# A router kernel on one core: a trip counter for the spare products, one address wrap per trip, and rows 52 to 62 in seven loads

## The chip, the cores and the metric

The kernel runs on one core of a Trainium2 chip. The metric is the device time of one execution in microseconds; the lower the better. A core has five engines with their own instruction queues: TensorE (PE in the profile; its weight loads are PEld), VectorE (DVE), ScalarE (ACT), GpSimd (POOL) and SyncE (SP). They wait for each other by semaphores only.

## The reference

Router logits of 8,192 tokens against 8 experts, and a softmax over the 8:

```python
# x: (16, 512, 1024) float32, router_weights: (1024, 8) float32
logits = np.matmul(x, router_weights)
exp_logits = np.exp(logits - np.max(logits, axis=-1, keepdims=True))
return (exp_logits / np.sum(exp_logits, axis=-1, keepdims=True)).astype(np.float32)
```

The work is the reading of x, 33.6 MB, and little arithmetic: each token is 1,024 numbers against an 8-column matrix.

## The kernel before

**Rows.** The tokens lie on 128 partitions with 64 tokens each. "Row" j means token j of every partition, so a row is 128 tokens of 1,024 numbers, 0.5 MB of float32. There are 64 rows (`J`), cut into 8 chunks (`KO`) of 128 columns.

**Loads.** `LOADS` lists how many rows each load carries: 4, then four of 8, four of 4, three of 2, five of 1, in order of rows; row 63 comes last in three `PIECES` of 4, 2 and 2 chunks. The first load (rows 0 to 3) goes through SyncE as float32 into `x_f32`, and ScalarE casts it. All the others are issued by GpSimd (L187, L200) one after the other at the start and are turned to bfloat16 on the way into `x_all`, where every row has its own place: no load waits for a buffer. SyncE waits for each load in turn (L175) and adds its number of rows to the semaphore `s_in`, which TensorE takes down by one before each row (L232).

**A row on TensorE.** The row has to be turned, so that the 1,024 columns lie on partitions: eight transposes (`loop_turn`), five into the PSUM tile `ptv`, three into `pts`. VectorE copies `ptv` to `xTv` (L421), ScalarE copies `pts` to `xTs` (L375). Then eight products with the weights `w_bf` accumulate the row's logits in `lg` (`multiply`). There are two buffers of each, so TensorE turns row j+1 before it multiplies row j.

**The loop.** Rows 1 to 62 are 31 trips (`TRIPS`) of two rows, written as basic blocks that only TensorE runs: `rows_turn` turns an odd row and multiplies the even one before it, `rows_even` turns an even row and branches back (L323), and `rows_multiply` runs two spare products and multiplies the odd row. The addresses are in registers: `r_x[c]` is where chunk c of the next row lies, `r_l` where the logits go. After each row all are advanced (L243, L247), and `r_l` is wrapped by a mask (L246), because `lg` has 16 places. In the trace neighbouring additions appear as one record, FUSED_REGOPS.

**Spare products.** `fill` multiplies constants (`filler`) into a bank that nobody reads. Two of them run in every trip. In addition the block `rows_spare` runs six in a straight line. It is entered after an odd row where the address in `r_x[0]` has certain bits (L319 masks it into `r_t`, L320 compares). `x_all` is laid at such an address (`ROW_AT`) that this holds just before rows 12, 20, 28 and 36, each the first row of the load that follows a load of eight.

**The softmax.** Every eight rows VectorE and ScalarE do the softmax of a group (peak, difference, exponential, sum, reciprocal, scaling) between their copies. After the loop come row 63 in pieces, the last four rows one by one, and two stores of the output by SyncE (L178, L180).

Of the kernel before, what the change touches and what calls it, by code (L numbers as in the profile page):

```python
# [11 lines left out]
def kernel(  # L12
# [6 lines left out]
    nc = tc.nc  # L19
    P = 128  # L20
    B, S, D = x.shape
# [3 lines left out]
    KO = D // P  # L25
    J = M // P
# [6 lines left out]
    bf16 = mybir.dt.bfloat16  # L33
    Exp = mybir.ActivationFunctionType.Exp
    X = mybir.AxisListType.X
    ALU = mybir.AluOpType

    LOADS = [4] + [8] * 4 + [4] * 4 + [2, 2, 2] + [1] * 5  # L40
    PIECES = [4, 2, 2]
    G, SKIP = 8, 4
    TRIPS = 31
# [5 lines left out]
    DONE = ends[-1]  # L49
    assert sum(LOADS) == J - 1 and sum(PIECES) == KO and ends[-1] == J - ALONE  # L50
    VN, SN = 5, 3

    LOT, SPARE = 8, 6
    ROW_AT = 32 - LOADS[0] - LOT
    assert LOADS[1:5] == [LOT] * 4 and 64 - ROW_AT == LOADS[0] + LOT * 5

    place = [16640]  # L60

    def sb(name, shape, dtype):
        size = mybir.dt.size(dtype)
        for n in shape[1:]:
            size *= n
        at = place[0]
        place[0] = -(-(at + size) // 64) * 64
        return nc.alloc_sbuf_tensor_at(name, shape, dtype, offset=at).ap()

    def ps(name, shape, dtype):  # L70
        return nc.alloc_psum_tensor(name, shape, dtype).ap()

    x_f32 = sb("x_f32", [P, LOADS[0], D], fp32)
    place[0] = X_AT = ROW_AT * D * 2
    xa = sb("x_all", [P, J, D], bf16)
    identity = sb("identity", [P, P], bf16)
    ident = sb("ident", [P, P], fp32)
    w8 = sb("w8", [KO, P, N], fp32)
# [31 lines left out]
    s_w = nc.alloc_semaphore("s_w")  # L110
    s_ld = [sem(f"s_ld{i}") for i in range(len(LOADS))]
    s_z = [sem(f"s_z{i}") for i in range(len(PIECES))]
# [21 lines left out]

    first = [sum(LOADS[:i]) for i in range(len(LOADS))]
    cols = [sum(PIECES[:i]) for i in range(len(PIECES))]
# [61 lines left out]
    for i, n in enumerate(PIECES):  # L198
        c = slice(cols[i] * P, (cols[i] + n) * P)
# [5 lines left out]
    pe = nc.tensor  # L205
    r_x = [pe.alloc_register(f"rx{c}") for c in range(KO)]
    r_l = pe.alloc_register("rl")
    r_t = pe.alloc_register("rt")
    for c, r in enumerate(r_x):

        pe.reg_mov(r, X_AT + D * 2 + c * P * 2 + (P - 1) * 2)
    pe.reg_mov(r_l, LG_AT + 256 * (SKIP - 1))

    def at(ap, like, r):
        return mybir.RegisterAccessPattern(
            ap=ap, dtype=like.dtype, memsetref=like.tensor.name + "_set",
            regref=r.name, is_regloc_offset=False, reg_ap_offset=r.name,
            const_ap_offset=0, const_sub_tensor_id=0,
        )

    def again(like, **k):
        return pe.add_instruction(copy.replace(like, name=f"I-{nc.next_id()}", **k))

    def turn_ap(b, c):
        return (ptv if c < VN else pts)[b][:, c if c < VN else c - VN, :]
# [4 lines left out]
    def loop_turn(b):  # L230

        pe.wait_ge(s_in, 1).then_inc(s_in, -1)  # L232
        for c in range(KO):
            t = again(
                turn_like,
                ins=(turn_like.ins[0], at([[J * D, P], [1, P]], xa, r_x[c])),
                outs=(pe.lower_ap(turn_ap(b, c), opt=False),),
            )
            if c == VN - 1:
                t.then_inc(s_tv, 1)  # L240
            if c == KO - 1:
                t.then_inc(s_ts, 1)
        pe.reg_add(r_l, r_l, 256)  # L243
        for c in range(KO):
            if c == KO // 2:
                pe.reg_alu(r_l, r_l, -4097, ALU.bitwise_and)  # L246
            pe.reg_add(r_x[c], r_x[c], D * 2)  # L247

    def turn(j):
        for c in range(KO):  # L250
            t = pe.transpose(turn_ap(j % 2, c), xa[:, j, c * P:(c + 1) * P], identity)
            if c == VN - 1:
                t.then_inc(s_tv, 1)
            if c == KO - 1:
                t.then_inc(s_ts, 1)
        return t

    def multiply(b, dst):

        for c in range(KO):  # L260
            if c == 0:
                pe.wait_ge(s_c[b], 2).then_inc(s_c[b], -2)
            if dst is None:
                m = again(
                    mult_like,
                    ins=(
                        pe.lower_ap(w_bf[:, c, :], opt=False),
                        pe.lower_ap(chunk(b, c), opt=False, for_matmul_weights=True),
                    ),
                    outs=(at([[2 * G * 64, P], [1, N]], lg, r_l),),  # L270
                    start_tensor_calc=(c == 0),
                    stop_tensor_calc=(c == KO - 1),
                )
            else:
                m = pe.matmul(  # L275
                    dst, lhsT=chunk(b, c), rhs=w_bf[:, c, :],
                    start=(c == 0), stop=(c == KO - 1),
                )
            if c == KO - 1:
                m.then_inc(s_p, 1)  # L280

    def fill():
        return pe.matmul(spare, lhsT=filler[:, 0:P], rhs=filler, start=True, stop=True)  # L283
# [5 lines left out]
    for n in range(N):  # L289
        t = pe.transpose(w_ps[:, n, :], w8[:, :, n], ident[0:KO, 0:KO])  # L290
# [2 lines left out]
    mult_like = fill().ins  # L293
    pe.wait_ge(s_idb, 1)
    pe.wait_ge(s_in, 1).then_inc(s_in, -1)  # L295
    turn_like = pe.transpose(turn_ap(0, 0), xa[:, 0, 0:P], identity).ins  # L296
    turn(0)
    pe.wait_ge(s_wb, 1)


# [4 lines left out]
    only_pe = OrderedEngineSet([pe.engine])  # L305
    nc.br("rows_turn", engines=only_pe)
    with nc.body("rows_spare", valid_engines=only_pe):
        for _ in range(SPARE):
            fill()
        pe.br("rows_even")  # L310
    with nc.body("rows_multiply", valid_engines=only_pe):
        fill()
# [3 lines left out]
    with nc.body("rows_turn", valid_engines=only_pe):  # L316
        loop_turn(1)
        multiply(0, None)
        pe.reg_alu(r_t, r_x[0], (64 + 32 + LOT - 1) * D * 2, ALU.bitwise_and)  # L319
        pe.br_eq(r_t, 32 * D * 2, on_true="rows_spare", on_false="rows_even")  # L320
    with nc.body("rows_even", valid_engines=only_pe):
        loop_turn(0)
        pe.br_lt(r_x[0], left_of(TRIPS - 1), on_true="rows_multiply", on_false="rows_done")  # L323
# [238 lines left out]
```

## Time and profile before

| | |
|---|---|
| median of 4 runs | 85.64 us (85.54 to 85.68) |
| profiled execution, its own time | 85.68 us |
| its span, first to last instruction | 84.4 us |
| PE busy / PEld busy | 69.8 us (83%) / 54.6 us (65%) |
| DVE busy / ACT busy | 39.4 us (47%) / 38.0 us (45%) |
| HBM read | 33.59 MB, 401 GB/s over the span |
| spare products in the trace | 85 records |
| loads issued by GpSimd | 16 and 3 pieces, from 2.7 to 14.0 us |

The profile's times are counted from the first instruction of the span. A line of its timeline gives the start, the time to the last end of the merged instructions, the engine, the line of the kernel, the operation, the tiles and the count; in brackets stands the idle time of the engine before it and what ended it. PEq is TensorE's sequencer: `PEq L232` is the wait for a row. A line of the waits gives the total in us, the number and the longest. A matmul's own duration is a latency: neighbours overlap, so what counts is the distance between starts. The busy time of the spare products is therefore more than what they take from others.

### The profile page before, as it was taken

The page shows a single profiled execution, that of the slowest core. Times are in us where ns is not written, and L with a number is a line of the kernel's source. Part 1 is how long each engine was busy: PE and PEld are TensorE (multiplying, and loading weights), DVE is VectorE, ACT ScalarE, POOL GpSimd, SP SyncE. Part 2 cuts the span into 40 slices and gives each one's busy share as a digit, 9 for nine tenths or more (in the row PEclk, how much of TensorE's full clock was granted, in tenths as well). Part 3 has the DMA queues.
Part 4 walks back from the last instruction along what each step waited for, and adds up shares of the span by engine and source line. Part 5 has one row for each costly group of instructions (what it writes and reads, how often), then busy time and mean ns, then how long its engine had stood idle before and what let it go on. Part 6 is the DMA issues. An engine that isn't in the chain of part 4 may idle for free. (4 is left out here: it accounts for less than half of the span.)

```text
span 84.4 us, 3030 instructions
## 1 busy us (share of the span) xinstructions
PE 69.8 (83%) x1118; PEld 54.6 (65%) x1118; DVE 39.4 (47%) x114; ACT 38.0 (45%) x81; POOL 11.3 (13%) x26
## 2 busy tenths in 40 slices
PE   0070376889999999999996999999999999999870
PEld 0040364759786788748881787678878888877650
DVE  0030042224364277527560476347657646765662
ACT  0600868323264255525451265426556544655580
POOL 0699996000000000000000000000000000000000
PEclk9999999999999999999999999999999999999999
DMA  5999979988998999799969999999999999999930
GB/s 148 388 458 264 225 148 249 249 186 186 249 249 171 202 249 241 155 225 249 233 148 229 198 233 202 233 202 225 206 214 200 214 216 214 204 208 211 187 117 11
DMA packets 3184, 18.12 MB, mean 215 GB/s; under 512 B 488, under 2 KB 1000, under 8 KB 2032
## 3 DMA queue, kind: packets, MB, share of 16 engines
q0 software_dynamic: 2736, 15.73, 90.4%
q1 hardware_dynamic: 432, 2.36, 7.4%
q10 hardware_dynamic: 16, 0.03, 0.2%
HBM read 33.59 MB, written 0.26 MB: 401 GB/s over the span
## 5 line engine op out<-in xcount | busy, mean ns | idle before, releaser
L421 DVE COPY xTv<-ptv 128x640 bf16<-128x640 bf16 x63 | 30.9, 491 | 33.0 <-PE ptv L296 27.7
L375 ACT COPY xTs<-pts 128x384 bf16<-128x384 bf16 x63 | 30.0, 476 | 35.2 <-PE pts L296 34.8
L296 PE MATMUL ptv<-identity,x_all 128*128 128x128 bf16 x311 | 29.3, 228 | 7.0 <-PEq L295 3.6
L283 PE MATMUL spare<-filler 128*128 128x512 bf16 x85 | 25.9, 402 | 0.1
L296 PEld LDWEIGHTS ptv<-identity,x_all 128*128 (+1 forms) x311 | 19.3, 100 | 9.1 <-issue 8.5
L296 PE MATMUL pts<-identity,x_all 128*128 128x128 bf16 x186 | 21.8, 229 | 0.0
L283 PEld LDWEIGHTS lg<-w_bf,xTv 128*128 128x128 bf16 x305 | 15.9, 99 | 8.1 <-issue 1.6
L283 PE MATMUL lg<-w_bf,xTv 128*128 128x8 bf16 x305 | 16.8, 168 | 0.0
L296 PEld LDWEIGHTS pts<-identity,x_all 128*128 x186 | 14.1, 104 | 0.0
L283 PE MATMUL lg<-w_bf,xTs 128*128 128x8 bf16 x183 | 13.2, 166 | 0.0
L283 PEld LDWEIGHTS spare<-filler 128*128 128x128 bf16 x85 | 6.1, 101 | 4.8 <-issue 0.6
L283 PEld LDWEIGHTS lg<-w_bf,xTs 128*128 128x128 bf16 x183 | 9.0, 96 | 0.0
L187 POOL DMA_DIRECT2D x_all<-in_x_dram x16 | 8.6, 598 | 2.2 <-POOLq L149 2.2
L361 ACT CAST x_all<-x_f 128x1024 bf16<-128x1024 f32 x4 | 4.0, 1044 | 5.2 <-ACTq L378 5.2
L290 PE MATMUL lg<-ident,w 8*128 8x8 f32 x8 | 1.0, 251 | 4.7 <-PEq L288 4.7
L290 PEld LDWEIGHTS lg<-ident,w 8*128 8x128 f32 x8 | 0.9, 197 | 4.7 <-issue 4.7
L441 DVE TENSOR_REDUCE mx<-lg 128x8 f32 x8 | 1.8, 224 | 4.4 <-DVEq L491 4.0
L412 DVE CAST identity<-ident 128x128 bf16<-128x128 f32 x1 | 0.5, 519 | 4.6 <-POOL ident L193 4.6
L364 ACT ACTIVATE ev<-ex 128x64 f32<-128x64 f32 x8 | 2.1, 256 | 1.4 <-DVE ex L441 0.8
L377 ACT ACT_TABLE_LOAD x1 | 1.3, 1283 | 2.2 <-PEq L149 2.2
L457 DVE TENSOR_REDUCE ssum<-ev 128x8 f32<-128x64 f32 x8 | 1.7, 218 | 0.0
L441 DVE TENSOR_TENSOR ex<-lg,mx 128x64 f32<-128x64 f32 x8 | 1.7, 215 | 0.0
(41 smaller groups left out, 16.0 us busy)
## 6 DMA issues: line engine op xcount, KB each, us to landing
x_all<-in_x_dram POOLq DMA_DIRECT2D x4, 2048.0 KB, 27.5
x_all<-in_x_dram POOLq DMA_DIRECT2D x4, 1024.0 KB, 51.6
x_f<-in_x_dram SPq DMA_DIRECT2D x1, 2048.0 KB, 8.5
x_all<-in_x_dram POOLq DMA_DIRECT2D x3, 512.0 KB, 62.0
x_all<-in_x_dram POOLq DMA_DIRECT2D x5, 256.0 KB, 66.1
out_dram<-out_all SPq DMA_DIRECT2D x1, 240.0 KB, 2.0
x_all<-in_x_dram POOLq DMA_DIRECT2D x1, 128.0 KB, 67.7
x_all<-in_x_dram POOLq DMA_DIRECT2D x2, 64.0 KB, 67.5
```

The lines of the kernel that those rows point to most:

```text
L187: nc.gpsimd.dma_start(out=xa[:, first[i]:first[i] + r, :], in_=x_rows[:, first[i]:first[i] + r, :]).then_inc(s_ld[i], 16)
L283: return pe.matmul(spare, lhsT=filler[:, 0:P], rhs=filler, start=True, stop=True)
L290: t = pe.transpose(w_ps[:, n, :], w8[:, :, n], ident[0:KO, 0:KO])
L296: turn_like = pe.transpose(turn_ap(0, 0), xa[:, 0, 0:P], identity).ins
L361: act.copy(xa[:, k, :], x_f32[:, k, :]).then_inc(s_cast, 1)
L364: return act.activation(ev, ex, func=Exp).then_inc(s_ev, 1)
L375: act.copy(xTs[j % 2], pts[j % 2][:, 0:SN, :]).then_inc(s_c[j % 2], 1)
L377: act.preload_act_table(Exp)
L412: dve.tensor_copy(out=identity, in_=ident).then_inc(s_idb, 1)
L421: dve.tensor_copy(out=xTv[j % 2], in_=ptv[j % 2][:, 0:VN, :]).then_inc(s_c[j % 2], 1)
L441: return dve.add_instruction(kind(name=f"I-{nc.next_id()}", engine=dve.engine, **k))
L457: dve.reduce_sum(ssum[:, :, 0], ev, axis=X).then_inc(s_d, 1)
```

## The change

- `LOADS` ends in 3, 2, 2 and four of 1 instead of 2, 2, 2 and five of 1: rows 52 to 62 come in seven loads instead of eight.
- `r_l` is wrapped only after odd rows (`b == 1`), so once in a trip.
- `r_t` becomes a counter. It starts at `STEP` = 3, loses 3 after each odd row, and below 1 the trip goes to `rows_spare`. There two spare products run, `r_t` gains 4, and the block repeats until `r_t` reaches 12: three pairs. The mask of the address (L319) goes. Past the lots of eight, `rows_last` sets the counter so high that it does not come to an end again.
- The visits of `rows_spare` thereby lie before rows 2, 10, 18, 26 and 34.
- `x_all` no longer needs a certain address: it is laid first, at 16,640 bytes, and `x_f32` after it.
- `turn(0)` gives the pattern instruction itself (`made`), and the transpose that was made ahead of it for that purpose goes.

```diff
-    LOADS = [4] + [8] * 4 + [4] * 4 + [2, 2, 2] + [1] * 5
+    LOADS = [4] + [8] * 4 + [4] * 4 + [3, 2, 2] + [1] * 4
...
-    LOT, SPARE = 8, 6
-    ROW_AT = 32 - LOADS[0] - LOT
-    assert LOADS[1:5] == [LOT] * 4 and 64 - ROW_AT == LOADS[0] + LOT * 5
+    LOT, STEP = 8, 3
+    LOTS = LOADS.count(LOT)
+    assert LOADS[1:1 + LOTS] == [LOT] * LOTS
...
+    X_AT = place[0]
+    xa = sb("x_all", [P, J, D], bf16)
     x_f32 = sb("x_f32", [P, LOADS[0], D], fp32)
-    place[0] = X_AT = ROW_AT * D * 2
-    xa = sb("x_all", [P, J, D], bf16)
...
     pe.reg_mov(r_l, LG_AT + 256 * (SKIP - 1))
+    pe.reg_mov(r_t, STEP)
...
         pe.reg_add(r_l, r_l, 256)
+        if b == 1:
+            pe.reg_add(r_t, r_t, -STEP)
         for c in range(KO):
-            if c == KO // 2:
+
+            if c == KO // 2 and b == 1:
                 pe.reg_alu(r_l, r_l, -4097, ALU.bitwise_and)
             pe.reg_add(r_x[c], r_x[c], D * 2)
 
     def turn(j):
+        made = None
         for c in range(KO):
             t = pe.transpose(turn_ap(j % 2, c), xa[:, j, c * P:(c + 1) * P], identity)
+            made = made or t.ins
...
-        return t
+        return made
...
-    turn_like = pe.transpose(turn_ap(0, 0), xa[:, 0, 0:P], identity).ins
-    turn(0)
+    turn_like = turn(0)
...
     with nc.body("rows_spare", valid_engines=only_pe):
-        for _ in range(SPARE):
-            fill()
+        fill()
+        fill()
+        pe.reg_add(r_t, r_t, LOT // 2)
+        pe.br_lt(r_t, LOT // 2 * STEP, on_true="rows_spare", on_false="rows_spared")
+    with nc.body("rows_spared", valid_engines=only_pe):
+        pe.br_lt(
+            r_x[0], X_AT + D * 2 * (LOADS[0] + (LOTS - 1) * LOT),
+            on_true="rows_even", on_false="rows_last",
+        )
+    with nc.body("rows_last", valid_engines=only_pe):
+        pe.reg_mov(r_t, J * STEP)
         pe.br("rows_even")
...
-        pe.reg_alu(r_t, r_x[0], (64 + 32 + LOT - 1) * D * 2, ALU.bitwise_and)
-        pe.br_eq(r_t, 32 * D * 2, on_true="rows_spare", on_false="rows_even")
+        pe.br_lt(r_t, 1, on_true="rows_spare", on_false="rows_even")
```

## The prediction

> **What bounds the kernel now.** First the page's slices, to see which resource never rests.
>
> ```profile
> PE   0070376889999999999996999999999999999870
> ...
> DMA  5999979988998999799969999999999999999930
> ```
>
> The 16 DMA engines are full from the second slice to the 38th; TensorE is also full from the ninth on, so being full tells nothing alone. Next SyncE's queue, which waits for every load and passes it on (L175), whole and then in four stretches (17.2 to 46.4 us, to 65.9, to 73.3, to 79.5):
>
> ```profile
> SPq L175 <- DMA x_all<-in_x_dram: 64.6, 16, 9.7
> ...
> SPq L175 <- DMA x_all<-in_x_dram: 29.1, 3, 9.7
> ...
> SPq L175 <- DMA x_all<-in_x_dram: 19.3, 4, 4.9
> ...
> SPq L175 <- DMA x_all<-in_x_dram: 7.3, 3, 2.5
> ...
> SPq L175 <- DMA x_all<-in_x_dram: 6.1, 5, 1.3
> ```
>
> Loads of 8, 4, 2 and 1 rows come 9.7, 4.8, 2.4 and 1.2 us apart: about 1.21 us a row without a pause. POOL issues all of them by 14 us and no issue waits for compute, so nothing that TensorE does can move the stream. Then TensorE's timeline at the places that the change touches:
>
> ```profile
> 11.82 0.22 PE L283 MATMUL lg<-w_bf,xTs 128*128 128x8 bf16 x3
> 13.49 0.69 PE L296 MATMUL ptv<-identity,x_all 128*128 128x128 bf16 x5 [1.45 <-PEq L232]
> ...
> 14.29 1.06 PE L283 MATMUL spare<-filler 128*128 128x512 bf16 x2
> 15.15 0.32 PE L283 MATMUL lg<-w_bf,xTv 128*128 128x8 bf16 x5
> ...
> 44.14 1.46 PE L283 MATMUL spare<-filler 128*128 128x512 bf16 x6
> 46.48 0.44 PE L296 MATMUL ptv<-identity,x_all 128*128 128x128 bf16 x5 [0.89 <-PEq L232]
> ...
> 78.37 0.44 PE L296 MATMUL ptv<-identity,x_all 128*128 128x128 bf16 x5
> ...
> 79.58 0.44 PE L296 MATMUL ptv<-identity,x_all 128*128 128x128 bf16 x5 [0.40 <-PEq L232]
> ```
>
> The last number that decides is the 0.40: row 62, the last of the loop, finds TensorE idle and waiting for its load (SyncE passes it on at 79.43). From there a fixed chain runs to the end at 84.4. So the end is the end of the DMA stream plus about 5 us, as long as TensorE has caught up by row 62. It has, narrowly: row 36 starts at 55.21 though SyncE had it at 51.16; row 52 at 69.83 (68.22); row 61 at 78.37 (78.20).
>
> **The change, part by part.** The profiled execution took 85.68 us, 84.4 of span and 1.3 around it; the median is 85.64, so I add changes to 85.64.
>
> *One load fewer in rows 52 to 62.* The same bytes in seven loads instead of eight. What a load costs beside its bytes is read from two stretches of the stream, 17.2 to 46.4 (8-row loads) and 73.3 to 79.4 (single rows):
>
> ```profile
> DMA packets 445, 6.27 MB, mean 215 GB/s; under 512 B 48, under 2 KB 48, under 8 KB 48
> ...
> q0 software_dynamic: 445, 6.27, 100.9%
> ...
> DMA packets 772, 1.25 MB, mean 206 GB/s; under 512 B 89, under 2 KB 223, under 8 KB 772
> ...
> q0 software_dynamic: 772, 1.25, 112.1%
> ```
>
> A row lands as 0.262 MB: 1.22 us at 215 GB/s, 1.27 at 206, so a load costs 0.05 us. The trace's packet records agree: the marks that close the single rows come 1.253 us apart, of pairs 2.458, of fours 4.867; 2 x 1.253 - 2.458 = 0.05 and 2 x 2.458 - 4.867 = 0.05. Hence three rows take 3 x 1.204 + 0.05 = 3.66 us, and row 62 and the pieces of row 63 come **0.05 us earlier**. From above: the packets' own times (172.9 ns for 2,048 B, 323.8 for 4,096) give 8 x (2 x 172.9 - 323.8) = 0.18 us, with the 22 ns mark 0.20; but the shares over 100% say that packets overlap, so I stay with the intervals. From below: a 6,144 B packet has no row here. If it were carried as three packets of 2,048 B, the load would cost 3 x 1.253 = 3.76, 0.10 more, and the stream would end 0.05 us later. Against this the sizes 512 to 16,384 B all lie on one line.
>
> The Trainium skill (DMA: Bandwidth & Descriptors, "Anatomy of one DMA") puts a fixed 2.0 us on each DMA of this path. By that rule a load fewer would be worth up to 2.0 us if loads ran one at a time, for 83.6; single rows landing 1.25 us apart exclude that here.
>
> *Where the regrouped rows arrive.* From SyncE's 65.80 for row 51: rows 52 to 54 at 69.46, 55 and 56 at 71.92, 57 and 58 at 74.38, 59 at 75.63. TensorE now takes rows 52, 55, 57 and 59 at 69.83, 72.84, 74.71 and 76.54: each is still there 0.3 us or more before it is wanted. Nothing, as long as TensorE is no earlier than now; if it is, it waits, and row 62 decides anyway. POOL's one issue fewer (0.6 us) ends work that nobody waits for.
>
> *Register work in the loop.* Per trip (two rows) the sequencer loses one address wrap and one mask, and gains one add:
>
> ```profile
> L246 PEldq ALU_OP  x62: 36/36/42, 11.0 to 79.7; - x62
> ...
> L319 PEldq ALU_OP  x31: 32/32/32, 11.7 to 78.9; - x31
> ...
> L323 PEldq COMPARE_BRANCH  x31: 76/208/218, 13.9 to 80.0; - x31
> ```
>
> A trip takes 1.83 us (48.96 to 50.80 between spare products). Its matrix work is 16 transposes of 0.0555 apart, 16 products of 0.025 and two spare ones of 0.216: 1.72. The rest is mostly a hole of 0.09 us before the two spare products, where the sequencer runs wrap, adds and the taken branch L323. The wrap holds it 0.10 us from its start to the next adds, so the hole goes: 1.74 us a trip, between 1.72 and (if the added add eats it) 1.83. From row 36 on that is 13 trips x 0.09 = 1.2 us less work for TensorE. Worth nothing at the end: it becomes waiting for loads.
>
> *The spare products.* Now six run before rows 12, 20, 28 and 36. The counter starts at 3, loses 3 a trip and is left at 12, so after the change they run before rows 2, 10, 18, 26 and 34. The first visit is new. Products of 512 columns come 0.43 us apart there (14.29 to 15.15; 0.216 from 23 us on), so six take 2.6 us from about 11.95, and row 2 starts at 14.55, not 13.49. Row 4 then starts some 0.35 us late (TensorE was idle 0.67 before it). This lateness ends at row 28 at the latest, where TensorE idles 0.89 us. It may also bring the fast rate earlier: the fast rate came at 22.9 us, after the first 3.4 us without a hole. That only lengthens the wait before a lot. The visit before row 34 instead of 36 leaves row 36 where it was.
>
> *The small loop.* A round adds an add and a taken branch (0.21 us by L323) under two products of 0.43 us together; with some 0.06 us either side of the branch, the round fits or overhangs by up to 0.1 us. Three rounds and two more branches: at most 0.5 us. It is exposed only before row 34, where TensorE is late, and covered by the 1.2 us above and the 0.40 idle before row 62. Without the 1.2 it would cost 0.1 us.
>
> The Trainium skill (Runtime: NRT & Kernel Launch, "Instruction fetch mechanics") speaks against more branches: one whose target is not in the instruction window stalls for a fetch. No such fetch appears in this trace after the start, and 31 taken branches cost 0.21 us each.
>
> The product dropped from `turn_like` lets row 0 go 0.1 us earlier, ahead of waits for row 2. The moved tiles keep their sizes and paths: no row prices a new address; I take nothing.
>
> Sum: -0.05 us: **85.59 us**.
>
> **The rivals.** *Packets count in full:* the stream is saved 0.20 us, 85.44. For: their own times. Against: equal intervals. *The load saves nothing* (its gap is filled, or the odd size costs 0.05 back): 85.64 to 85.69. *TensorE loses its fast rate near the end, slower:* being ahead, it waits more (7 trips x 1.74 = 12.2 us of work in the last 14.4). In the rows from 12.70 to 19.50 it was busy 2.61 and 2.73 of 3.40 us and stayed at half rate, a trip taking 2.98 us (18.09 to 21.07) against 2.49 for two loads. Each such trip loses 0.49 us; it decides once the loss passes the 0.40 idle before row 62, so from the last trip or two; two trips, 0.6 us net: 86.2. Against: 0.89 us idle before row 28 left the products at full rate.
>
> **How the numbers follow.** Forecast 0.58, nothing saved 0.12, packets in full 0.15, rate lost 0.15. About 0.2% (0.17 us) is what a measurement of this kernel can tell from no change; the four runs lie within 0.14. The first two cases are "within", less 0.02 on either side for layout and launch: same 0.66, faster 0.17, slower 0.17. The range 85.42 to 85.82 takes in the first three cases, and a little of the last.
>
> **What would show it.** Right: SyncE passes row 62 on 0.05 us earlier, the three-row load 3.66 us after row 51's, TensorE still idle there, 30 spare products of visits with the first six at about 12 us, a trip near 1.74 us. Wrong: no idle time before row 62, or transposes of 311 ns late in the span, or a three-row load of 3.8 us or more.

## The result and the profile after

The changed kernel takes **85.74 us** (median of 48 runs, 85.62 to 86.0) against 85.61 for the kernel before (71 runs). The ratio is 1.0016 with a 95% interval of 1.0012 to 1.0021: 0.13 us *slower*. That lies within 0.2% and inside the predicted range, but the forecast was 0.05 us *less*, and the interval excludes a gain.

The span, however, became shorter. First the page's head and DMA slices of the kernel after:

```profile
span 84.1 us, 3010 instructions
...
DMA  5999969989997999699969999999999999999930
```

The profiled execution took 85.66 us with a span of 84.09 (84.087 in the trace): 1.57 us lie around the span. Before it was 85.68 with 84.36: 1.32. The other executions agree. Those in the table come each with a time and a span (given to 0.1 us), so the two can be told apart without the profile's details:

| | executions | mean time less span, us | mean span, us |
|---|---|---|---|
| before, in five comparisons | 19 to 35 each | 1.318 to 1.326 | 84.33 to 84.41 |
| after | 50 | 1.566 (standard deviation 0.03) | 84.19 |

So the span lost 0.1 us by its medians (84.3 before, 84.4 in one of the five comparisons, 84.2 after; the means, 0.14 to 0.22 apart, hold some long executions of before), and 0.25 us came on outside it. That loss is the whole surprise. The rest of the profile did in the main what the prediction said. SyncE's wait for the loads after, whole and then from 17.0 to 46.2 us (eight rows), to 65.7 (four), to 74.3 (the three-row load and two pairs) and to 79.3 (single rows); columns: time waited, times, longest:

```profile
SPq L173 <- DMA x_all<-in_x_dram: 64.6, 15, 9.7
...
SPq L173 <- DMA x_all<-in_x_dram: 29.0, 3, 9.7
...
SPq L173 <- DMA x_all<-in_x_dram: 19.3, 4, 4.9
...
SPq L173 <- DMA x_all<-in_x_dram: 8.5, 3, 3.6
...
SPq L173 <- DMA x_all<-in_x_dram: 4.9, 4, 1.3
```

The longest wait of the fourth stretch is the three-row load: 3.6 us. The packet records give 3.67 from the mark of row 51 (the 4 B packet that closes its load) to the mark of this load (3.66 was predicted). A 6,144 B packet took 474 ns, halfway between 324 for 4,096 B and 625 for 8,192: the odd size costs nothing of its own. From the mark of the last eight-row load to that of row 62 it is 33.064 us after and 33.106 before, **0.042 us less** (0.05 was predicted). The experiments below bear it out: nearly all of their kernels have 33.106 with eight loads and 33.057 or 33.058 with seven, 0.048 less.

TensorE's timeline after, at the first visit, before row 28 and at the end of the loop:

```profile
11.62 0.22 PE L287 MATMUL lg<-w_bf,xTs 128*128 128x8 bf16 x3
11.74 2.74 PE L287 MATMUL spare<-filler 128*128 128x512 bf16 x6
14.28 0.56 PE L254 MATMUL ptv<-identity,x_all 128*128 128x128 bf16 x5
...
46.26 0.44 PE L254 MATMUL ptv<-identity,x_all 128*128 128x128 bf16 x5 [1.16 <-PEq L231]
...
55.30 0.59 PE L287 MATMUL spare<-filler 128*128 128x512 bf16 x2
...
57.03 0.59 PE L287 MATMUL spare<-filler 128*128 128x512 bf16 x2
...
58.75 0.60 PE L287 MATMUL spare<-filler 128*128 128x512 bf16 x2
...
78.07 0.44 PE L254 MATMUL ptv<-identity,x_all 128*128 128x128 bf16 x5
...
79.35 0.44 PE L254 MATMUL ptv<-identity,x_all 128*128 128x128 bf16 x5 [0.48 <-PEq L231]
```

The new visit's six products stand before row 2 at 11.74 us, and row 2 follows at 14.28. The idle time before row 28 grew from 0.89 to 1.16 us. A trip, from one spare pair to the next, is 1.73 us instead of 1.83. Row 62 still finds TensorE idle, for 0.48 us instead of 0.40. And the register work, from the views of the lines L248 (wrap) and L314 (the loop's branch); count, shortest/median/longest in ns, first and last start:

```profile
L248 PEldq ALU_OP  x31: 36/36/42, 10.8 to 78.2; - x31
...
L314 PEldq COMPARE_BRANCH  x15: 76/207/208, 11.9 to 52.3; - x15
```

The wraps are halved (62 before), and the loop's 15 branches cost 208 ns at most, and the last starts at 52.3 us. They are hidden: TensorE still waits for loads behind them, 0.48 us before row 62.

### The profile page after: what moved, and what is told of

Read it like the earlier page. It is cut to its first block, busy times and chain, and to the rows that moved or that the text cites. A ratio compares the mean times of both kernels' runs of the same rounds, so it can differ in the third digit from the quotient of the medians.

```text
span 84.1 us, 3010 instructions
## 1 busy us (share of the span) xinstructions
PE 67.9 (81%) x1123; PEld 53.3 (63%) x1123; DVE 39.4 (47%) x114; ACT 38.0 (45%) x81; POOL 10.8 (13%) x25
## 5 line engine op out<-in xcount | busy, mean ns | idle before, releaser
L254 PE MATMUL ptv<-identity,x_all 128*128 128x128 bf16 x315 | 28.3, 221 | 8.8 <-PEq L231 5.3
L287 PE MATMUL spare<-filler 128*128 128x512 bf16 x91 | 27.2, 400 | 0.0
L254 PE MATMUL pts<-identity,x_all 128*128 128x128 bf16 x189 | 21.2, 222 | 0.0
L287 PEld LDWEIGHTS lg<-w_bf,xTv 128*128 128x128 bf16 x305 | 15.3, 97 | 7.2
L287 PE MATMUL lg<-w_bf,xTv 128*128 128x8 bf16 x305 | 16.5, 167 | 0.0
L254 PEld LDWEIGHTS pts<-identity,x_all 128*128 (+1 forms) x189 | 13.5, 99 | 0.0
L287 PEld LDWEIGHTS spare<-filler 128*128 128x128 bf16 x91 | 6.8, 100 | 4.3 <-issue 1.4
L185 POOL DMA_DIRECT2D x_all<-in_x_dram x15 | 8.1, 595 | 2.2 <-POOLq L147 2.2
```

Source lines behind the costliest of these rows:

```text
L185: nc.gpsimd.dma_start(out=xa[:, first[i]:first[i] + r, :], in_=x_rows[:, first[i]:first[i] + r, :]).then_inc(s_ld[i], 16)
```

## The experiments

All compare with the kernel before on the same chip. "Around" is the mean of time less span over the run's executions, "profiled" the same difference of its one profiled execution.

### Which part of the change, and is it the way out of the program?

The first theories: the new basic blocks lengthen the end of the program on the other engines (SyncE's way out above all), or the loads or the new loop do it.

**Loads alone.** The kernel before with one line changed:

```diff
-    LOADS = [4] + [8] * 4 + [4] * 4 + [2, 2, 2] + [1] * 5
+    LOADS = [4] + [8] * 4 + [4] * 4 + [3, 2, 2] + [1] * 4
```

> The kernel before with one edit alone: rows 52 to 62 in seven loads. Theory (blocks): every basic block leaves one instruction in each engine's program, and SyncE runs those of all later blocks after its last wait, outside the span, at about 0.125 us each (time less span is 1.32 us before, with 9 such instructions, and 1.57 after, with 11). Here there are 9 again, so time less span stays 1.32 us, the span falls by 0.05 us, and the median is 85.56 us, ratio 0.9994. Rival (loads): the new grouping itself is what slows the end; then the ratio is the 1.0016 of the whole change. Rival (placement of x_all at 16,640 bytes): not in this kernel, so the ratio is 0.9994 as well.

Measured: 85.64 us against 85.67, ratio 0.9995 (0.9979 to 1.0011); around 1.304 us, span 84.34 (before 84.41). The load grouping is harmless, and the lost 0.25 us isn't its doing.

**The six products in a straight line**, in the kernel after:

```diff
     with nc.body("rows_spare", valid_engines=only_pe):
-        fill()
-        fill()
-        pe.reg_add(r_t, r_t, LOT // 2)
-        pe.br_lt(r_t, LOT // 2 * STEP, on_true="rows_spare", on_false="rows_spared")
-    with nc.body("rows_spared", valid_engines=only_pe):
+        for _ in range(6):
+            fill()
+        pe.reg_add(r_t, r_t, LOT // 2 * STEP)
         pe.br_lt(
```

> The kernel after with the six spare products in a straight line again (the counter gains 12 at once): one basic block and the small loop are gone, everything else of the change stays. Theory (blocks): SyncE has 10 instructions behind its last wait, so time less span is 1.45 us and the median 85.62 us, ratio to before 1.0001. Rival (small loop): the loop of pairs costs the 0.13 us inside the span; then the span falls by 0.13 or more, time less span stays 1.57, ratio 1.000. Rival (placement): nothing changes, 85.74 us, ratio 1.0016. The times of theory and first rival are near each other; time less span tells them apart.

Measured: 86.54 us, ratio 1.0077 (1.0047 to 1.0106). The time around the span is back at 1.308 us, but the span is 85.13: a second effect, of its own. (Two of the twelve executions, 85.56 and 85.78 us, are without it.) From the DMA part of this kernel's page:

```profile
q8 instruction: 1, 0.02, 0.1%
...
out_dram<-out_all SPq DMA_DIRECT2D x1, 240.0 KB, 4.4
```

The same store in the kernel after, which has no q8 line:

```profile
out_dram<-out_all SPq DMA_DIRECT2D x1, 240.0 KB, 2.0
```

One transfer of 16 KB of instructions lies in the span, at 82.59 us. It is a single packet of 1.04 us. The landing of the first store is told by 16 updates of its semaphore: 15 come by 82.75 us, the last at 85.12, behind the transfer, so the store lands 4.4 us after its issue instead of 2.0. That this last part waited for the transfer on the same DMA engine is a reading of these times; the records don't name the engine. SyncE's last wait shows it, in this kernel and then in the kernel after:

```profile
SPq L180 <- DMA out_dram<-out_all: 2.1, 1, 2.1
```

```profile
SPq L180 <- DMA out_dram<-out_all: 1.1, 1, 1.1
```

One microsecond more at the very end, with the stream unchanged.

**More blocks.** The kernel before with blocks behind its last product that only TensorE runs:

```diff
+    nc.br("more0", engines=only_pe)
+    for k in range(4):
+        with nc.body(f"more{k}", valid_engines=only_pe):
+            pe.reg_mov(r_t, 0)
+            pe.br(f"more{k + 1}" if k < 3 else "more_done")
+    nc.switch_bb("more_done")
```

> The kernel before with five more basic blocks at the end, which only TensorE has work in (a register move and a branch each, after its last product). SyncE's program grows by five instructions behind its last wait; nothing else changes. Theory (blocks): time less span grows by 5 x 0.125 = 0.63 us to 1.95, the span stays, the median is 86.2 us, ratio 1.0073. Rivals (loads, placement, small loop): no change, 85.61 us, ratio 1.000.

Measured: 85.63 us, ratio 0.9991 (0.997 to 1.0011); around 1.323 us. The trace has none of the moves and branches, and as many records of TensorE's sequencer as before. So nothing of the addition shows as having run, and this kernel can't tell what a block costs.

**SyncE's part last.** In the kernel after, SyncE's waits and stores (L169 to L180) are written behind the last block, so SyncE has no blocks after its last wait.

> The kernel after with SyncE's waits and stores written behind the last basic block instead of ahead of the first one. SyncE then passes the 11 instructions of the blocks near 2 us, when it has nothing to do until 9.5 us, and has none behind its last wait. Theory (blocks): time less span falls by 11 x 0.125 = 1.4 us to about 0.2, the span stays at 84.1 to 84.2, the median is 84.4 us, ratio 0.985. If another engine's way out takes over, it is less: VectorE and ScalarE end at 82.6 and 81.9 us and have few blocks left, so they should not. Rivals (loads, placement, small loop): 85.74 us, ratio 1.0016.

Measured: 85.89 us, ratio 1.0019 (0.9999 to 1.0038); around 1.567 us, exactly as after. SyncE's way out isn't it, and the first theory falls for SyncE. The way out of the other engines isn't tested here.

### Is it the length of TensorE's program?

The second theory: the place where TensorE's program ends, relative to some boundary. Three kernels add spare products to the kernel after, and one takes three away from the kernel before:

```diff
     mult_like = fill().ins
+    for _ in range(1):   # 2 and 3 in the next two
+        fill()
```

```diff
-    LOT, SPARE = 8, 6
+    LOT, SPARE = 8, 3
```

> The kernel after with one more spare product on TensorE at the start (a weight load and a product, in the 3.5 us in which TensorE has nothing to do before row 0): its program is 226 instructions long instead of 224 (229 before). Theory (program length): what the change costs lies outside the span (1.32 us before, 1.57 after, over 50 and 35 runs) and comes from where TensorE's program ends against a 16 KB block of code; five instructions make 0.25 us. Then time less span is about 1.47 us here, the span stays. Rival (control flow): the small loop and its two extra blocks make the 0.25 us, whatever the length; then it stays 1.57 us.

> As the run before, with two more spare products: 228 instructions on TensorE. Theory (program length): time less span about 1.37 us, median 85.55 us, below the 85.61 to 85.67 of the kernel before. Rival (control flow): 1.57 us and 85.74.

> With three more spare products: 230 instructions on TensorE, as many as in the run with six spare products in a straight line, whose span was a microsecond longer in most executions with a 16 KB instruction transfer at 82.6 us beside the first store of the output. Theory (program length): time less span 1.3 us, and the transfer appears in the span, so the median is about 86.5 us. Rival (control flow): 1.57 us, no transfer, 85.74.

> The kernel before with three spare products instead of six in the straight line of the visits: TensorE's program is 223 instructions instead of 229, with the control flow, loads and placement of before. TensorE gains 0.65 us at each of four visits, all ahead of waits for loads. Theory (program length): time less span rises from 1.32 to about 1.6 us, the span stays, median 85.9 us, ratio 1.003. Rival (control flow): time less span stays 1.32 us, ratio 1.000.

| | us | ratio (95%) | around | span |
|---|---|---|---|---|
| 1 product more | 85.88 | 1.002 (1.0 to 1.0041) | 1.582 | 84.30 |
| 2 more | 85.85 | 1.0001 (0.9974 to 1.0029) | 1.579 | 84.27 |
| 3 more | 85.88 | 1.0036 (1.0019 to 1.0054) | 1.586 | 84.36 |
| before, 3 fewer in the block | 85.62 | 0.9997 (0.9987 to 1.0006) | 1.323 | 84.31 |

(The ratios are those on record and not the quotients of the medians: 85.85 against 85.64 would be 1.0025.) Products change nothing outside the span, in either kernel. The second theory falls.

### Is it the loop, or the branches?

**Straight six, with the extra block kept** (as the second experiment, but `rows_spared` stays a block of its own):

> The kernel after with six spare products in a straight line, but the block rows_spared kept as a block of its own: all blocks of the change, no block that branches back to itself. Time less span has been 1.57 us in every kernel with the small loop and 1.31 in every kernel without, whatever the length of the program. Theory (self-loop: a block of TensorE that branches to itself costs 0.25 us outside the span): 1.31 us here. Rival (number of branches in TensorE's program, 6 after, 4 or 5 in all kernels at 1.31): 5 here, so 1.31 as well. Rival (number of blocks): 1.57. The span is that of the earlier straight line, 84.3 us, or 85.3 where the 16 KB instruction transfer meets the stores.

Measured: 86.58 us, ratio 1.0107 (1.0074 to 1.0139); around 1.320 us, span 85.29 with the 16 KB transfer at 81.75 us. As the second experiment. Its trace has as many records of TensorE's sequencer, 375, so the block by itself added nothing that ran.

**The loop, with fewer branches.** In the kernel after `rows_spared` goes straight to `rows_even` and `rows_last` is taken out, so that there are also visits before rows 42, 50 and 58:

> The kernel after without the test of rows_spared: the small loop stays and always goes on to rows_even, so there are also visits before rows 42, 50 and 58 (six spare products each, 1.3 us of TensorE). TensorE's program has 5 branches instead of 6. Theory (self-loop): time less span 1.57 us. Rival (number of branches): 1.31 us. The span may grow by up to 0.9 us, because the last visit lies 4 rows before the end of the loop; only time less span is read.

Measured: 87.59 us, ratio 1.0213 (1.0183 to 1.0243). The span of 86.33 is the extra visits': TensorE is late and starts row 62 at 81.64 us without an idle time. Around: 1.315 us, *with* the loop. So the loop isn't it.

**More branches without a loop.** The kernel before with three compare-branches behind its last product:

```diff
+    nc.br("more0", engines=only_pe)
+    for k in range(3):
+        with nc.body(f"more{k}", valid_engines=only_pe):
+            pe.br_lt(
+                r_x[0], 5 + k, on_true=f"more{k + 2}" if k < 2 else "more_done", on_false=f"more{k + 1}"
+            )
+    with nc.body("more3", valid_engines=only_pe):
+        pe.br("more_done")
+    nc.switch_bb("more_done")
```

> The kernel before with three compare-and-branch instructions on TensorE after its last product, none of them backward: 7 branches in its program, no self-loop. Theory (self-loop): time less span 1.32 us, median 85.64. Rival (number of branches, 6 or more): 1.57 us, median 85.89.

Measured: 86.0 us, ratio 1.0032 (1.0018 to 1.0046); around **1.584 us**, span 84.38. The whole effect, with the loads, the loop and the counter of the kernel before.

**A loop at the end.** The kernel before with a block behind its last product that adds to `r_x[0]` and branches to itself for three rounds:

> The kernel before with a small loop on TensorE after its last product: one block with a register add and a branch to itself, run three times (under 1 us, while VectorE and ScalarE finish and the stores run; 5 branches in its program). Theory (self-loop): time less span 1.57 us, span unchanged, median 85.89. Rival (number of branches): 1.32 us, 85.64.

Measured: 86.47 us, ratio 1.0083 (1.0057 to 1.011); around 1.407 us, in between. The span of 85.10 holds the 16 KB transfer, at 83.12 us.

By now the theory was the number of branches in the program: four before, more in each kernel that showed the effect. Four runs to test that:

**Everything but the new control flow.** The kernel before with the seven loads, one wrap per trip and no extra transpose, so with the branches of before:

```diff
-            if c == KO // 2:
+            if c == KO // 2 and b == 1:
...
-    turn_like = pe.transpose(turn_ap(0, 0), xa[:, 0, 0:P], identity).ins
-    turn(0)
+    turn_like = turn(0)
```

> Everything of the change that does not touch the control flow, on the kernel before: seven loads for rows 52 to 62, one address wrap per trip, the extra transpose gone; the visits of six spare products stay as before, TensorE's program keeps 4 branches. Theory (branches in TensorE's program: up to 5 give 1.32 us outside the span, 6 and 7 give 1.57): time less span 1.32 us, the span 0.05 to 0.1 us shorter than before, median 0.05 to 0.1 us below the kernel before, ratio 0.9988 to 0.9994. Rival (length of the program decides, with branches counting as several instructions): 1.32 as well.

**Two branches more** than before (as the three above, with `range(2)`):

> The kernel before with two compare-and-branch instructions on TensorE after its last product: 6 branches, nothing else of the change. Theory (branches): time less span 1.57 us, span unchanged, no instruction transfer in the span, ratio 1.003. Rival (something else of the kernel after, such as visits or counter): 1.32, ratio 1.000.

**A longer program**, the kernel before with 16 products of 8 columns at its start:

> The kernel before with 16 products of 8 columns at the start, where TensorE has 3.6 us to spare: 249 instructions in its program without the marks of blocks instead of 217 (261 instead of 229 with them), 4 branches. Theory (number of branches, not length): time less span 1.32, no instruction transfer in the span, ratio 1.000. Rival (length decides, a branch counting as about ten instructions): three branches' worth longer, so 1.57 us, or 1.32 with a 16 KB transfer in the span and a span up to 1 us longer.

**Five branches, shorter.** The straight-line kernel with two products per visit instead of six:

> The straight-line kernel with 5 branches (86.5 us, a 16 KB instruction transfer beside the stores), with two spare products per visit instead of six: 8 instructions shorter, 209 instead of 217, TensorE idle 0.9 us more ahead of each lot. Theory (number of branches): the transfer stays, span 85.2, median 86.5, time less span 1.32. Rival (length decides, branches counting as about ten): the end of the program moves 8 instructions away from the border, so no transfer, span 84.2 to 84.3, time less span 1.32, median 85.6.

| | us | ratio (95%) | around | profiled | span |
|---|---|---|---|---|---|
| all but the control flow | 85.74 | 1.0013 (1.0 to 1.0025) | 1.458 | 1.475 | 84.30 |
| two branches more | 85.81 | 1.0018 (1.0009 to 1.0028) | 1.461 | 1.468 | 84.35 |
| 16 small products more | 86.05 | 1.0043 (1.0028 to 1.0058) | 1.337 | 1.321 | 84.70 |
| straight, two per visit | 85.57 | 0.9992 (0.9982 to 1.0002) | 1.329 | 1.308 | 84.26 |

The first row ends the theory: with the branches of before, and 31 wraps and a transpose fewer, 0.13 us of the effect is there (the seven loads had proved harmless). The longer program has the 16 KB transfer (82.33 us) and its later end, but not the effect outside the span. The straight kernel with two per visit has neither. It also shows something that it wasn't made for. Three stretches of its profile; the columns behind the engines are granted clock, DMA share and GB/s:

```profile
26.70:30.10 3.40, 3.10 (x36) 2.57 (x37) 1.17 (x4) 0.61 (x2) 0.00 (x0) 0.50 1.06 226
47.20:50.60 3.40, 3.40 (x37) 2.57 (x36) 1.65 (x6) 1.49 (x4) 0.00 (x0) 0.50 1.09 227
50.60:54.00 3.40, 3.40 (x66) 2.73 (x65) 1.71 (x5) 1.44 (x3) 0.00 (x0) 1.00 0.97 202
```

TensorE fell to half its clock twice, for 3.4 us each time, and the span (84.26) is as short as any: TensorE's speed in the middle doesn't set the end.

### Is it the number of instructions that TensorE's sequencer executes?

What the additions (branches) and the removals (wraps) have in common is the number of instructions that the sequencer executes. Counted in each trace are its records without weight loads: branches, register operations, moves, semaphore instructions. Products, which had proved harmless, aren't in it. The changed kernel has 47 register operations fewer than before, 17 branches and two moves more: 428 before, 400 after. Set out by the count, all the kernels above fall into an order if the count is taken modulo 32:

| count mod 32 | kernels (count) | profiled time less span, us |
|---|---|---|
| 3 | the loop with fewer branches (419) | 1.313 |
| 12 | before, loads alone, more blocks, 3 products fewer, 16 small products more (428) | 1.309 to 1.322 |
| 13 | all but the control flow (397) | 1.475 |
| 14 | two branches more (430) | 1.468 |
| 15 | three branches more (431) | 1.573 |
| 16 | after, SyncE last, 1 to 3 products more (400) | 1.567 to 1.575 |
| 18 | loop at the end (434) | 1.394 |
| 23 | straight six, both forms; straight, two per visit (375) | 1.307 to 1.308 |

This order was found after the fact, so two kernels tested it: the kernel after, with register operations at its start that change nothing.

```diff
     pe.reg_mov(r_t, STEP)
+    for _ in range(5):   # 14 in the second
+        pe.reg_alu(r_t, r_t, -1, ALU.bitwise_and)
```

> The kernel after with five register operations that change nothing (r_t AND -1) at the start, where TensorE waits until 4.6 us. The profiled executions give time less span to a few ns: 1.31 to 1.32 us where TensorE's sequencer ran 375, 419 or 428 instructions beside weight loads and products, 1.39 at 434, 1.47 at 397 and 430, 1.57 at 400 and 431. Theory (count): taken modulo 32 (23, 3, 12; 18; 13 and 14; 16 and 15) this is one bump around 15, so what counts is where the sequencer's count stands when the program ends, not what the instructions are. Here the count is 405, 21 modulo 32: time less span 1.31 us, the span as after, 84.1 to 84.3, median 85.45 to 85.55, ratio 0.998 to 0.999: faster than both kernels, with five instructions more than after. Rival (6 branches cost 0.25 us, 5 or fewer as far as they go): 1.57 us, 85.74 to 85.9.

> As before with fourteen register operations: the count is 414, that is 30 modulo 32 and 14 modulo 16. Theory with a period of 32: time less span 1.31 us. Theory with a period of 16, which fits the kernels so far as well: 1.47 us. Rival (branches): 1.57 us. The operations take about 1.3 us from 3.0 us on and end before TensorE's first wait does; the span stays, unless the 16 KB instruction transfer shows up beside the stores.

| | count, mod 32 | us | ratio (95%) | around | profiled | span |
|---|---|---|---|---|---|---|
| 5 more | 405, 21 | 85.69 (before 85.61) | 1.0005 (0.9996 to 1.0013) | 1.472 | 1.474 | 84.22 |
| 14 more | 414, 30 | 85.59 | 0.999 (0.9969 to 1.0011) | 1.303 | 1.307 | 84.27 |

The 14 extra operations, by their line in the trace, and the granted clock and span of that kernel:

```profile
L213 PEldq ALU_OP  x14: 32/32/42, 3.2 to 4.4; - x14
...
core 0: 84.1 us, clock 0.988
```

They run at the start, in time that nobody waits for. The kernel with *more* work is 0.15 us faster than the kernel after: 1.303 around the span, the short span kept. So nothing in the change's loads, addresses, loop, blocks or branches costs 0.25 us by itself, since this kernel has them all. The five-operation kernel missed its forecast of 1.31 and gave 1.474, so the raised stretch is wider than the table suggested: from 13 to 21.

What is shown is that the time outside the span moves with the register operations and branches of TensorE's sequencer, and that it can be moved both ways without touching the work. What stays open: why, the exact shape (the period of 32 rests on these kernels alone, and within the stretch 1.394 at 18 lies below 1.474 at 21), and whether the count of executed instructions or something that goes with it decides. Since every span comes from a recorded execution, it is open too whether the recording has a part in it.

Where the extra time lies, the traces tell for three kernels. They hold semaphore updates outside the span as well, and the last nine, of one semaphore, form a group of their own. It begins 1.07 to 1.09 us behind the last instruction in all ten kernels with 1.31 to 1.32. With all but the control flow and with five operations more (1.47) it begins at 1.24, with the loop at the end (1.39) at 1.16: later by just what their time outside the span is longer, 0.17 and 0.07 us. There the loss lies behind the span. In the kernel after (1.57), in the other kernels like it and with two branches more (1.47) the group begins at 1.07 to 1.08 as in the first ten, and no record shows where their extra time lies. So the raised kernels aren't all of one kind.

## Why the prediction was wrong

**Right in its steps within the span.**

- *The stream.* One load fewer was to bring row 62 0.05 us earlier: 0.042. The bound by packet times, 0.20, and with it the rival that packets count in full, is out. So is the odd size's 0.10 us: 3.67 us, not 3.76.
- *The trip* came out at 1.73 us for 1.74. *The first visit* was to stand at 11.95 us and row 2 at 14.55: 11.74 and 14.28. Full rate came earlier, at 14.5 us by the clock's record instead of 23.0, and only lengthened the waits, as said: 1.16 us before row 28. Row 4, which was to start some 0.35 us late, waited 0.85 us for its load instead.
- *The loop* was to be hidden until row 34: its last branch starts at 52.3 us.
- *The rate near the end* was not lost: transposes in the last rows take as long as before (0.44 us for five), and the 0.48 us before row 62 are the spare time that the rival needed gone. The straight kernel with two products per visit did lose the rate, in mid-span, and paid nothing: the rival's own condition, that only the last trip or two count, fits that.
- *The end follows row 62 by about 5 us:* 79.19 to 84.09 us, 4.90; before 79.43 to 84.36, 4.93.

**The step that failed** is the first sentence of the sum: "The profiled execution took 85.68 us, 84.4 of span and 1.3 around it; the median is 85.64, so I add changes to 85.64." That takes the 1.3 as a constant. It was 1.57. With 0.1 us less of span (by the medians) and 0.25 us more around it, the sum is 0.15 us more; 0.13 was measured. For a change of the 1.3 the prediction kept only a chance of "0.02 on either side for layout and launch", without a row behind it: one profile can't show how its own surroundings would change. The row that would have bounded it is the difference between time and span in kernels with other instruction counts, and the trace of before alone had none. That 85.74 lies in the predicted range is in part luck: a loss that the sum lacked is partly offset by a larger gain in span than it had.

The gain in span is larger than the stream's 0.042 us. The kernels with the seven loads, compared with the kernel before on the same chip, have spans shorter by 0.03 to 0.14 us (but for those with the late transfer or extra visits). In the profiled executions the mark of the first eight-row load comes between 16.28 and 16.49 us (16.41 before, 16.29 after), so what of the gain is more than the 0.042 is not settled.

**The rule on branches.** The prediction weighed the Trainium skill (Runtime: NRT & Kernel Launch, "Instruction fetch mechanics"), by which a taken branch out of the window stalls for a fetch, against 0.21 us for a taken branch. The trace after agrees with the row: 201 to 208 ns, and no fetch in the span. (Of the prediction's 31 branches 30 are taken; the last ends the loop and takes 76 ns.) But the same section says that instructions come in blocks of 16 KiB and that the crossing is mostly hidden. The straight-line kernel has a fetch that isn't: a 16 KB transfer 1.04 us long beside the last stores, and a span 0.8 us longer (85.13 against 84.33 for the kernel after with SyncE last, in the same comparison).

## What to carry to other kernels

Take the time and the span of every execution apart before explaining a difference of a few tenths of a microsecond: here the work became faster and the execution slower. A change of control flow or register work alone moved the time around the span here by up to 0.26 us, in either direction, so a small edit is judged by its span, and by a twin with a few idle register operations more. What a DMA load costs beside its bytes is read from the intervals between marks in a busy stream (0.05 us), not from the packets' own times, which overlap.

No version beat both kernels clearly. The straight kernel with two products per visit (ratio 0.9992), the kernel after with 14 idle operations (0.999) and the loads alone (0.9995) all have intervals that hold 1 against the kernel before.

## What was not expected of the hardware

- The time outside the span: 1.30 to 1.34 us by the means of ten kernels and 1.41 to 1.59 of the ten others, moved by register operations and branches of TensorE's sequencer. Within one kernel every execution lies within 0.06 us of the mean, which is little more than the rounding of the span.
- The transfer of 16 KB of instructions at 81.8 to 83.1 us, in four kernels: it is a single packet of 1.04 to 1.83 us. Straight six (both forms), the loop at the end and the 16 small products have it. A straight kernel with four products fewer hasn't, nor has the kernel after with three products more. Which length or way of branching brings it into the span is open.
- The granted clock: it came to full at 14.5 us after the new visit of 2.7 us without a hole. In the kernels with a visit before row 2 it came between 13.1 and 15.5 us, in those without between 16.5 and 23.0. In the straight kernel with two products per visit it went back to half twice, for 3.4 us each time: at 26.7 us, within an idle time of 2.02 us before row 12, and at 47.2, 0.8 us after one of 2.02 us before row 28. Idle times of 1.80 us before row 4 and 0.90 before row 20 left it at full.
